# Input i of the second layer as seven block products, with VectorE's order written out through i and g

## The chip, the cores and the metric

One core of a Trainium2 chip runs the whole kernel. The metric is the device time of one execution in microseconds (us). The kernel before takes 673.21 us, the median of three runs (673.01 to 674.18).

## What is computed

A trunk of two layers on 512 tokens of width 1024, in float32. Each layer is `h = h + norm(mixer(norm(h)))`, followed by a gated embedding. Layer 0's mixer is attention, layer 1's is a gated linear recurrence (HGRN2). What the change touches is the input projection of layer 1:

```
u = rms_norm(h, norm_pre[1])
proj = u @ w_in                      # 512x1024 times 1024x4096
q, fl, inp, g = split(proj, 4)       # four blocks of 1024 columns
...
o = recurrence(q, fl, inp)
y = (norm(o) * silu(g)) @ w_out
```

`i` below is `inp`, the third block of columns; `g` is the fourth. Both are wanted with tokens on the partitions ("token major"), and both are 512x1024 times 1024x1024 products.

## The kernel before, in words

**Float32 products.** Every operand is kept as a pair of rounded values, hi and lo. `split` (L272) makes a pair with a copy on ScalarE (hi) and a subtraction on VectorE (lo). `three` (L138) multiplies a pair by a pair in three matmuls: L140 takes hi and w_hi, L141 takes lo and w_hi, L142 takes hi and w_lo. Weights come in chunks of 128x1024: `fetch` (L112) issues a DMA on SyncE's queue, and `load_w` (L117) splits the chunk into w_hi (ScalarE, L273) and w_lo (VectorE, L274). There are two buffers for w_hi and two for w_lo, so that a chunk is split only after the chunk two places before it has been used.

**The normed x.** The norm's factor of each token, `r1`, is not multiplied in ahead of i and g: the products run on `xg = h * gain` (tiles b2h, b2l) and the result is scaled by `r1` while it is moved out of PSUM. For the later products with q and fl, `scaled_norm` (L285) makes the normed x itself, `u` (b1h, b1l), from a factor that `spread` (L255) has laid out over the partitions: one VectorE instruction (un, L288), one ScalarE copy (hi) and one VectorE subtraction (lo) for each of eight slices k.

**The tail of layer 0** (`layer_tail`, L339) makes the new h: the gate is multiplied slice by slice (o = 0 to 7), and `gated` (L387) computes sigmoid, product, sum, then `nxt` makes the slice of xg (L281, L282) and adds its squares to the running sum ss_acc (`Stat.add`, L220). The last four slices come one after the other out of 24 matmuls each (`lin_a`).

**i** is made by `lin_b_tok` (L188) in two halves of 96 matmuls, each half with four chunks of weights that serve 24 matmuls apiece. Between the halves the column sums of ss_acc (L236) give `r1`; `spread` (L259) stands after the first chunk of the second half.

**g** is made by `gates` (L783) with seven products of half-size blocks in place of eight (the Strassen-Winograd scheme, here called p1, p2, p3, p6, p7, p4, p5 in the order of the program). Each product is 24 matmuls on two chunks of weights (12 matmuls apiece) into two PSUM banks out of the ring psB of six (L78). Four of the seven (p3, p6, p7, p5) have sums of x blocks as their operand, the tiles `as`, made by `pair` (L721): two ScalarE scalings, four VectorE sums of 128x256 and a split for each of four k; the sums are made in tsum1, which is then used again for weights. Three of the products have sums of weight blocks: the sums are made in tsum0 and tsum1, by DMAs on GpSimd's queue that add to what is there (`more`, L780) and, once for each of two chunks, by a VectorE addition (L818: t2s = t1 + b22). `plus` (L788) combines the products on VectorE, `end` (L793) scales with `r1` and applies SiLU on ScalarE.

**Order.** Within `tc.manual_schedule(engines=...)` the named engines keep the order of the program; elsewhere a planner orders each engine's instructions. Around i and g only TensorE's order is written out before the change; the tail has a part (L371) in which VectorE's is. `pair` and `scaled_norm` are issued after i's matmuls and before `gates`.

The first product after g is that of fl for head 0 (psA<-b1h,w_f).

Of the kernel before, what the change touches and what calls it, by code (L numbers as in the profile page):

```python
# [10 lines left out]
F32 = mybir.dt.float32  # L11
# [35 lines left out]
def tile_fox_hgrn2(  # L47
# [56 lines left out]
    def col(c):  # L104
        return vecs[:, c:c + 1]
# [230 lines left out]
            with first(o == KT - 1):  # L336
                ac.activation(out=self.zg[o], in_=b, func=AF.Copy, scale=col(C_NPOST[self.layer] + o))

    def layer_tail(layer, h, ah, zg, last=False):  # L339

        st = ah.st = Stat()
        ah.zg, hm = zg, ah.mem
        for g in ah.begun:
            for _ in g:
                pass
        for o in range(len(ah.begun), KT - 1):
            eng = gp if not last and o == len(ah.begun) else ve
            for _ in ah.out(o, load_w(wo[layer, o], eng=eng)):
                pass
        eb = []  # L350
        fill = Fill()
        fill.add(*[ah.embed(o, eb.append) for o in LATE])
        with tc.manual_schedule(engines={PE}):
            for _ in ah.out(KT - 1):
                pass
            st.most()
            fill.run(2)
            with first():
                rs = st.rstd()
            fill.run(4)  # L360
            with first():
                rb = spread(rs, copy=False)
            fill.run()

        ws = [load_w(wgC[layer, c]) for c in range(2)]
        raws = [fetch(wgC[layer, c]) for c in range(2, 4)]

        def low(k):
            ve.tensor_tensor(out=hm[1][k], in0=h[k], in1=hm[0][k].bitcast(F32), op=ALU.subtract)

        with tc.manual_schedule(engines={DVE}):  # L371
            for k in range(KT):
                with first():
                    t = t2("zn")
                    ve.tensor_tensor(out=t, in0=rb, in1=zg[k], op=ALU.mult)
                    ve.tensor_tensor(out=h[k], in0=h[k], in1=t, op=ALU.add)
                    ac.copy(hm[0][k], h[k])
                    if k:
                        low(k - 1)
                if k in (4, 6):  # L380
                    ws.append(load_w(None, raw=raws[k // 2 - 2]))
            with first():
                low(KT - 1)
        for o, b in zip(LATE, eb):
            ac.copy(ah.ple(o), b)

        def gated(o, b, f=slice(0, S)):  # L387
            sg = t2("sgm")[:, f]
            ac.activation(out=sg, in_=b[:, f], func=AF.Sigmoid)  # L389
            ve.tensor_tensor(out=sg, in0=sg, in1=ah.ple(o)[:, f], op=ALU.mult)  # L390
            ve.tensor_tensor(out=h[o][:, f], in0=h[o][:, f], in1=sg, op=ALU.add)
            if last:
                nc.sync.dma_start(out[o][:, f], h[o][:, f])
            else:
                nxt(o)

        if not last:
            xg = pair_big("b2")
            stn = Stat()

            def nxt(o):
                split_scaled(xg[0][o], xg[1][o], h[o], col(C_NPRE[1] + o))
                stn.add(h[o])

        banks = lin_c(ws, hm)
        ws = [load_w(wgA[layer, o]) for o in range(2)]
        for o, b in enumerate(banks):
            gated(o, b)
        for o in range(4, KT):
            w = ws.pop(0)  # L410
            if last and o == KT - 1:

                for i in range(2):
                    f = slice(i * S // 2, (i + 1) * S // 2)
                    b = psA()
                    for k in range(KT):
                        three(b[:, f], (kcols(w[0], k), kcols(w[1], k)), (hm[0][k][:, f], hm[1][k][:, f]), k == 0, k == KT - 1)
                    gated(o, b, f)
            else:
                b = lin_a(w, hm)  # L420
                if o + 2 < KT:
                    ws.append(load_w(wgA[layer, o - 2]))
                gated(o, b)
        return None if last else (xg, stn)
# [293 lines left out]

        return (l1, sums)[q].tile([P, D], F32, name=f"tsum{q}{c}", tag=f"tsum{q}{c}")

    def pair(k):  # L721
        un = []
        for b in (k, k + 4):
            un.append(t2("un"))
# [6 lines left out]
        ve.tensor_tensor(out=sm[:, SM_G, :], in0=a12, in1=sm[:, SM_E, :], op=ALU.add)  # L731
        split(a_sum[0][k], a_sum[1][k], sm)

    xg, st = layer_tail(0, h, ah, slots("b3h", F32))

# [31 lines left out]
                three(banks[t], (hi[:, c], lo[:, c]), (w[0][:, f], w[1][:, f]), k == 0, k == 3)  # L769
        return banks  # L770

    def block(i, j, c):

        return wB1[8 + 4 * j + 2 * i + c]

    def more(dst, ap):

# [2 lines left out]

    CH = range(2)

    def gates(dst):  # L783

        def C(i, j, t):
            return dst[2 * (2 * i + t) + j]
# [5 lines left out]
        def end(i, j):  # L792
            for t in CH:  # L793
                q = 2 * i + t
                ac.activation(out=C(i, j, t), in_=C(i, j, t), func=AF.Silu, scale=r1[:, q:q + 1])

        def loads(raws):
            return [load_w(None, raw=raw) for raw in raws]

        t1 = [tsum(0, c) for c in CH]  # L800
        for c in CH:
            nc.sync.dma_start(t1[c], block(0, 0, c))
        w = loads(t1)
        for c in CH:
            more(t1[c], block(0, 1, c))
        p1 = product((0, 0), w)
        w = [load_w(block(1, 0, c)) for c in CH]
        for t in CH:
            ac.copy(C(1, 0, t), p1[t])
        p2 = product((0, 1), w)  # L810
        b22 = [fetch(block(1, 1, c)) for c in CH]
        w = loads(b22)
        plus(0, 0, p2, (1, 0))
        end(0, 0)
        p3 = product(SM_G, w)
        t2s = [tsum(1, c) for c in CH]
        for c in CH:
            ve.tensor_tensor(out=t2s[c], in0=t1[c], in1=b22[c], op=ALU.add)  # L818
            more(b22[c], block(0, 1, c))
        w = loads(t2s)  # L820
        p6 = product(SM_E, w)
        for c in CH:
            more(t2s[c], block(1, 0, c))
        w = loads(b22)
        plus(1, 0, p6, (1, 0))
        plus(0, 1, p3, (1, 0), ALU.subtract)
        p7 = product(SM_F, w)
        w = loads(t2s)
        plus(1, 1, p7, (1, 0))
        p4 = product((1, 1), w)  # L830
        w = loads(t1)
        plus(1, 0, p4, (1, 1))
        end(1, 0)
        p5 = product(SM_D, w)
        for i in CH:
            plus(i, 1, p5, (i, 1), (ALU.add, ALU.subtract)[i])
            end(i, 1)

    def evac_tok(half, banks):
        for t in range(NT):  # L840
            ac.activation(out=it[2 * t + half], in_=banks[t], func=AF.Copy, scale=r1[:, t:t + 1])

    with tc.manual_schedule(engines={PE}):
        banks = lin_b_tok(wB1[0:4], xg, 0)
        r1 = st.rstd()
        rb = []
        banks1 = lin_b_tok(wB1[4:8], xg, 1, between=lambda: rb.append(spread(r1)))
        evac_tok(0, banks)
        for k in range(4):
            pair(k)  # L850
        evac_tok(1, banks1)
        for k in range(KT):
            scaled_norm(u, k, h[k], C_NPRE[1], rb[0])
        gates(sg)
    att.close()

    y = pair_big("b2")
# [308 lines left out]
    with tc.If(ok > 0) as cmp:  # L1166
        with tc.tile_pool(name="rec", bufs=2) as rp:
            ah = bounded(rp)
        layer_tail(1, h, ah, it, last=True)
    with cmp.Else():  # L1170
        with tc.tile_pool(name="rec", bufs=2) as rp:
            general(rp)
# [6 lines left out]
        for o in EARLY:  # L1179
            for _ in ah.early(o):  # L1180
                pass
        layer_tail(1, h, ah, it, last=True)


_INS = ["xT", "pT", "vec", "wfl", "wA0", "wB0", "wA1", "wB1", "wo", "wgC", "wgA", "wpl"]
# [61 lines left out]
```

## Time and profile before

| | us |
|---|---|
| median of three runs | 673.21 |
| the profiled execution | 673.19 |
| its span, first to last instruction | 671.4 |
| TensorE busy | 654.9 |
| VectorE busy | 462.9 |
| ScalarE busy | 352.5 |

The granted clock of TensorE is 0.998 of full speed over the span. The profiled execution stands within 0.02 us of the median, and 1.8 us of it lie outside the span. In the rows below PE is TensorE, DVE VectorE, ACT ScalarE, POOL GpSimd and SPq SyncE's queue of DMAs. Times are us from the start of the span; a row of the timeline gives start and duration, and in brackets how long the engine was idle before it and what ended that. Durations of neighbours overlap on one engine, so what an instruction takes of the engine is read from one start to the next.

### The profile page before, as it was taken

The numbers are of one execution on the slowest core, as the hardware profiler recorded it, in microseconds if no ns is written. First come the engines' busy times: TensorE is split into PE (matmuls) and PEld (weight loads), VectorE is DVE, ScalarE is ACT, GpSimd is POOL, SyncE is SP. The second block draws the span as 40 slices with busy tenths as digits, with TensorE's granted clock in tenths as the row PEclk, the third lists the DMA queues.
The fourth block names the chain that finished last, engine by engine and source line by source line (L and its number), as shares of the span: only waits on it lengthen the run. The fifth ranks groups of instructions, "written<-read, shape, count | busy, mean of one in ns | idle before, by whom it ended". The sixth has DMA issues, their size and how long they took to land. (4 is left out here: it accounts for less than half of the span.)

```text
span 671.4 us, 8969 instructions
## 1 busy us (share of the span) xinstructions
PE 654.9 (98%) x3202; PEld 544.1 (81%) x3202; DVE 462.9 (69%) x935; ACT 352.5 (52%) x676; POOL 44.6 (7%) x51
## 2 busy tenths in 40 slices
PE   8999999999999998999999997999999998999996
PEld 5888888888888877888888876888888887888885
DVE  7596223888888897337699465669888888333953
ACT  6457223766767685434577454364445455434431
POOL 0101200000000061001000101100010000001000
PEclk9999999999999999999999999999999999999999
DMA  8322336655555575321223335721222224122131
GB/s 283 124 70 65 119 103 189 163 152 133 152 139 139 149 225 166 95 95 38 93 90 97 109 77 122 162 95 62 64 79 80 64 94 144 44 95 95 62 111 51
DMA packets 27156, 75.33 MB, mean 112 GB/s; under 512 B 3872, under 2 KB 4256, under 8 KB 27104
## 3 DMA queue, kind: packets, MB, share of 16 engines
q1 hardware_dynamic: 26240, 71.54, 34.6%
q0 software_dynamic: 864, 3.15, 2.7%
q8 instruction: 27, 0.44, 0.3%
q14 instruction: 25, 0.20, 0.1%
HBM read 59.86 MB, written 2.10 MB: 92 GB/s over the span
## 5 line engine op out<-in xcount | busy, mean ns | idle before, releaser
L140 PE MATMUL psA<-b1h,w_hi 128*128 128x512 f32 (+1 forms) x384 | 154.6, 403 | 0.0
L274 DVE TENSOR_TENSOR w_lo<-w_raw,w_hi 128x1024 fp32r<-128x1024 f32 x89 | 109.1, 1226 | 61.5 <-ACT w_hi L273 56.1
L142 PE MATMUL psA<-b1l,w_hi 128*128 128x512 f32 (+1 forms) x384 | 148.6, 387 | 0.0
L141 PE MATMUL psA<-b1h,w_lo 128*128 128x512 f32 (+1 forms) x384 | 148.2, 386 | 0.2 <-DVE w_lo L274 0.2
L273 ACT CAST w_hi<-w_raw 128x1024 fp32r<-128x1024 f32 x90 | 94.1, 1047 | 39.3 <-PE psB L141 17.2
L142 PEld LDWEIGHTS psA<-b1l,w_hi 128*128 128x128 f32 x384 | 72.1, 188 | 15.1
L140 PEld LDWEIGHTS psA<-b1h,w_hi 128*128 128x128 f32 x384 | 72.3, 188 | 12.9 <-ACT sgm L389 0.7
L141 PEld LDWEIGHTS psA<-b1h,w_lo 128*128 128x128 f32 x384 | 72.4, 189 | 12.7 <-DVE w_lo L274 0.6
L142 PE MATMUL psB<-w_lo,b2h 128*128 128x512 f32 x120 | 46.9, 391 | 2.3 <-DVE w_lo L274 2.3
L621 ACT ACTIVATE pp<-pp,nm 128x128 f32<-128x128 f32 (+3 forms) x64 | 36.2, 565 | 23.0 <-DVE nm L619 22.2
L140 PE MATMUL psB<-w_hi,b2h 128*128 128x512 f32 x120 | 47.2, 395 | 0.0
L141 PE MATMUL psB<-w_hi,b2l 128*128 128x512 f32 x120 | 46.7, 389 | 0.0
L619 DVE CUSTOM_DVE_ANT_0 pp<-psB,cmask 128x128 f32<-128x128 f32 (+3 forms) x64 | 30.7, 479 | 14.5 <-PE psB L638 11.4
L230 DVE TENSOR_TENSOR ss_acc<-ss_acc,sq 128x512 f32<-128x512 f32 x26 | 17.9, 688 | 29.0 <-ACT sq L226 28.8
L140 PE MATMUL psA<-b2h,w_hi 128*128 128x512 f32 x80 | 31.8, 397 | 0.0
L274 DVE TENSOR_TENSOR PTl<-psB,PTh 128x128 fp32r<-128x128 f32 (+3 forms) x64 | 30.8, 481 | 1.0 <-ACT PTh L273 0.8
L142 PE MATMUL psA<-b2l,w_hi 128*128 128x512 f32 x80 | 31.2, 390 | 0.0
L638 PE MATMUL psB<-ident,pp 128*128 128x128 f32 x160 | 28.4, 276 | 2.8 <-DVE pp L624 1.5
L141 PE MATMUL psA<-b2h,w_lo 128*128 128x512 f32 x80 | 31.2, 390 | 0.0
L273 ACT CAST PTh<-psB 128x128 fp32r<-128x128 f32 (+3 forms) x64 | 26.9, 422 | 5.8 <-PE psB L638 4.9
L142 PEld LDWEIGHTS psB<-w_lo,b2h 128*128 128x128 f32 x120 | 22.5, 188 | 7.5 <-DVE w_lo L274 2.7
L624 DVE TENSOR_SCALAR pp<-pp,rden 128x128 f32<-128x128 f32 (+3 forms) x64 | 27.3, 426 | 1.0
(247 smaller groups left out, 1295.0 us busy)
## 6 DMA issues: line engine op xcount, KB each, us to landing
w_raw<-in_wA_dram SPq DMA_DIRECT2D x40, 512.0 KB, 3.3
w_raw<-in_wB_dram SPq DMA_DIRECT2D x19, 512.0 KB, 3.8
w_raw<-in_wo_dram SPq DMA_DIRECT2D x16, 512.0 KB, 4.0
h<-in_xT_dram SPq DMA_DIRECT2D x16, 256.0 KB, 6.3
h<-kh SPq DMA_DIRECT2D x32, 128.0 KB, 2.3
w_raw<-in_wgC_dram SPq DMA_DIRECT2D x8, 512.0 KB
w_raw<-in_wgA_dram SPq DMA_DIRECT2D x8, 512.0 KB, 3.3
h<-qh SPq DMA_DIRECT2D x16, 128.0 KB, 2.3
```

Source lines behind the costliest of these rows:

```text
L140: pe.matmul(out=out_ps, lhsT=sta[0], rhs=mov[0], start=start, stop=False)
L141: pe.matmul(out=out_ps, lhsT=sta[1], rhs=mov[0], start=False, stop=False)
L142: pe.matmul(out=out_ps, lhsT=sta[0], rhs=mov[1], start=False, stop=stop)
L230: ve.tensor_tensor(out=self.acc, in0=self.acc, in1=sq, op=ALU.add)
L273: ins = ac.copy(dst_hi, src)
L274: eng.tensor_tensor(out=dst_lo, in0=src, in1=dst_hi.bitcast(F32), op=ALU.subtract)
L619: ve.tensor_tensor_reduce(out=pp[:, :W], in0=sc[:, :W], in1=cmask[:, S - W:S], op0=ALU.add, op1=ALU.min, scale=1.0, scalar=-NEG, accum_out=nm)
L621: ac.activation(out=pp[:, :W], in_=pp[:, :W], func=AF.Exp, bias=nm, scale=-1.0, accum_out=den)
L624: ve.tensor_scalar(out=pp[:, :W], in0=pp[:, :W], scalar1=rden, scalar2=None, op0=ALU.mult)
L638: pe.transpose(out=tp[:, kt * P:(kt + 1) * P], in_=pp[:, kt * P:(kt + 1) * P], identity=ident)
```

## The change

i is made as g is: `gates` becomes `token_major(m, ...)`, called with m = 0 for i and m = 1 for g. `pair` moves into the tail of layer 0, each k right behind the slice h[k + 4] that it needs; of xg[0..3] only the first half of the tokens is made. t2s is loaded with block (1, 1) and t1 is added to it by an accumulating DMA from SBUF to SBUF, in place of the VectorE addition. `rstd` (the sums over ss_acc) stands after p1 of i, `spread` after p3 of i. `scaled_norm` is issued for two k at a time at four places of g: after p3, p6, p7 and p4. VectorE's order is that of the program through both.

```diff
--- before.py
+++ after.py
@@ -336,8 +336,10 @@
             with first(o == KT - 1):
                 ac.activation(out=self.zg[o], in_=b, func=AF.Copy, scale=col(C_NPOST[self.layer] + o))
 
-    def layer_tail(layer, h, ah, zg, last=False):
+    def layer_tail(layer, h, ah, zg, pair=None):
+        last = pair is None
         st = ah.st = Stat()
         ah.zg, hm = zg, ah.mem
         for g in ah.begun:
@@ -399,8 +401,12 @@
             stn = Stat()
 
             def nxt(o):
-                split_scaled(xg[0][o], xg[1][o], h[o], col(C_NPRE[1] + o))
+                f = slice(0, S // 2 if o < 4 else S)
+                split_scaled(xg[0][o][:, f], xg[1][o][:, f], h[o][:, f], col(C_NPRE[1] + o))
                 stn.add(h[o])
+                if o >= 4:
+                    pair(h, o - 4)
 
         banks = lin_c(ws, hm)
         ws = [load_w(wgA[layer, o]) for o in range(2)]
@@ -718,7 +724,7 @@
 
         return (l1, sums)[q].tile([P, D], F32, name=f"tsum{q}{c}", tag=f"tsum{q}{c}")
 
-    def pair(k):
+    def pair(h, k):
         un = []
         for b in (k, k + 4):
             un.append(t2("un"))
@@ -731,7 +737,7 @@
         ve.tensor_tensor(out=sm[:, SM_G, :], in0=a12, in1=sm[:, SM_E, :], op=ALU.add)
         split(a_sum[0][k], a_sum[1][k], sm)
 
-    xg, st = layer_tail(0, h, ah, slots("b3h", F32))
+    xg, st = layer_tail(0, h, ah, slots("b3h", F32), pair)
 
 
 
@@ -769,9 +775,9 @@
                 three(banks[t], (hi[:, c], lo[:, c]), (w[0][:, f], w[1][:, f]), k == 0, k == 3)
         return banks
 
-    def block(i, j, c):
-        return wB1[8 + 4 * j + 2 * i + c]
+    def block(m, i, j, c):
+        return wB1[8 * m + 4 * j + 2 * i + c]
 
     def more(dst, ap):
 
@@ -780,7 +786,7 @@
 
     CH = range(2)
 
-    def gates(dst):
+    def token_major(m, dst, between=None):
 
         def C(i, j, t):
             return dst[2 * (2 * i + t) + j]
@@ -792,66 +798,80 @@
         def end(i, j):
             for t in CH:
                 q = 2 * i + t
-                ac.activation(out=C(i, j, t), in_=C(i, j, t), func=AF.Silu, scale=r1[:, q:q + 1])
+                ac.activation(out=C(i, j, t), in_=C(i, j, t), func=AF.Silu if m else AF.Copy, scale=r1[:, q:q + 1])
 
         def loads(raws):
             return [load_w(None, raw=raw) for raw in raws]
 
         t1 = [tsum(0, c) for c in CH]
+        t2s = [tsum(1, c) for c in CH]
         for c in CH:
-            nc.sync.dma_start(t1[c], block(0, 0, c))
+            nc.sync.dma_start(t1[c], block(m, 0, 0, c))
         w = loads(t1)
         for c in CH:
-            more(t1[c], block(0, 1, c))
+            more(t1[c], block(m, 0, 1, c))
         p1 = product((0, 0), w)
-        w = [load_w(block(1, 0, c)) for c in CH]
+        w = [load_w(block(m, 1, 0, c)) for c in CH]
+        if between:
+            between(0)
         for t in CH:
             ac.copy(C(1, 0, t), p1[t])
         p2 = product((0, 1), w)
-        b22 = [fetch(block(1, 1, c)) for c in CH]
+        b22 = [fetch(block(m, 1, 1, c)) for c in CH]
         w = loads(b22)
+        for c in CH:
+            nc.sync.dma_start(t2s[c], block(m, 1, 1, c))
+            more(t2s[c], t1[c])
         plus(0, 0, p2, (1, 0))
         end(0, 0)
         p3 = product(SM_G, w)
-        t2s = [tsum(1, c) for c in CH]
         for c in CH:
-            ve.tensor_tensor(out=t2s[c], in0=t1[c], in1=b22[c], op=ALU.add)
-            more(b22[c], block(0, 1, c))
+            more(b22[c], block(m, 0, 1, c))
         w = loads(t2s)
+        if between:
+            between(1)
         p6 = product(SM_E, w)
         for c in CH:
-            more(t2s[c], block(1, 0, c))
+            more(t2s[c], block(m, 1, 0, c))
         w = loads(b22)
         plus(1, 0, p6, (1, 0))
         plus(0, 1, p3, (1, 0), ALU.subtract)
+        if between:
+            between(2)
         p7 = product(SM_F, w)
         w = loads(t2s)
         plus(1, 1, p7, (1, 0))
+        if between:
+            between(3)
         p4 = product((1, 1), w)
         w = loads(t1)
         plus(1, 0, p4, (1, 1))
         end(1, 0)
+        if between:
+            between(4)
         p5 = product(SM_D, w)
         for i in CH:
             plus(i, 1, p5, (i, 1), (ALU.add, ALU.subtract)[i])
             end(i, 1)
 
-    def evac_tok(half, banks):
-        for t in range(NT):
-            ac.activation(out=it[2 * t + half], in_=banks[t], func=AF.Copy, scale=r1[:, t:t + 1])
-    with tc.manual_schedule(engines={PE}):
-        banks = lin_b_tok(wB1[0:4], xg, 0)
-        r1 = st.rstd()
-        rb = []
-        banks1 = lin_b_tok(wB1[4:8], xg, 1, between=lambda: rb.append(spread(r1)))
-        evac_tok(0, banks)
-        for k in range(4):
-            pair(k)
-        evac_tok(1, banks1)
-        for k in range(KT):
+    r1 = None
+    rb = []
+    def beside_i(n):
+        nonlocal r1
+        if n == 0:
+            r1 = st.rstd()
+        if n == 1:
+            rb.append(spread(r1))
+    def beside_g(n):
+        for k in ((), (0, 1), (2, 3), (4, 5), (6, 7))[n]:
             scaled_norm(u, k, h[k], C_NPRE[1], rb[0])
-        gates(sg)
+    with tc.manual_schedule(engines={PE, DVE}):
+        token_major(0, it, beside_i)
+        token_major(1, sg, beside_g)
     att.close()
 
     y = pair_big("b2")
@@ -1166,7 +1186,7 @@
     with tc.If(ok > 0) as cmp:
         with tc.tile_pool(name="rec", bufs=2) as rp:
             ah = bounded(rp)
-        layer_tail(1, h, ah, it, last=True)
+        layer_tail(1, h, ah, it)
     with cmp.Else():
         with tc.tile_pool(name="rec", bufs=2) as rp:
             general(rp)
@@ -1179,7 +1199,7 @@
         for o in EARLY:
             for _ in ah.early(o):
                 pass
-        layer_tail(1, h, ah, it, last=True)
+        layer_tail(1, h, ah, it)
 
 
 _INS = ["xT", "pT", "vec", "wfl", "wA0", "wB0", "wA1", "wB1", "wo", "wgC", "wgA", "wpl"]
```

## Rows read from the trace of the kernel before

**Rows 1.** The page, busy time of the engines.

```profile
PE 654.9 (98%) x3202; PEld 544.1 (81%) x3202; DVE 462.9 (69%) x935; ACT 352.5 (52%) x676; POOL 44.6 (7%) x51
```

**Rows 2.** Windows i, g: length; PE, PEld, DVE, ACT, POOL busy; clock; DMA.

```profile
353.20:399.05 45.85, 45.84 (x210) 37.89 (x209) 33.17 (x51) 27.97 (x40) 3.01 (x2) 1.00 0.31 94
399.05:442.20 43.15, 39.12 (x169) 31.26 (x168) 26.12 (x27) 19.95 (x23) 4.47 (x6) 1.00 0.55 123
```

**Rows 3.** Waits of TensorE in both windows: total, times, longest.

```profile
PE psB L142 <- DVE w_lo L274: 4.0, 2, 2.3
```

**Rows 4.** Timeline of VectorE before those two waits.

```profile
402.14 1.23 DVE L818 TENSOR_TENSOR tsum<-tsum,w_raw 128x1024 f32<-128x1024 f32 x1 [5.36 <-DMA tsum<-in_wB_dram]
403.28 1.22 DVE L274 TENSOR_TENSOR w_lo<-tsum,w_hi 128x1024 fp32r<-128x1024 f32 x1
404.42 1.22 DVE L274 TENSOR_TENSOR w_lo<-w_raw,w_hi 128x1024 fp32r<-128x1024 f32 x1
...
412.31 1.23 DVE L818 TENSOR_TENSOR tsum<-tsum,w_raw 128x1024 f32<-128x1024 f32 x1 [3.05 <-DMA w_raw<-in_wB_dram]
```

**Rows 5.** Timeline of TensorE: i, then g's p3.

```profile
373.67 0.39 PE L142 MATMUL psA<-w_lo,b2h 128*128 128x512 f32 x1
...
375.03 0.39 PE L142 MATMUL psB<-w_lo,b2h 128*128 128x512 f32 x1
375.26 0.95 PE L236 MATMUL psB<-ones,ss_acc 128*128 128x1 f32 x8
...
415.06 0.39 PE L140 MATMUL psB<-w_hi,as 128*128 128x512 f32 x1
...
416.69 0.40 PE L141 MATMUL psB<-w_hi,as 128*128 128x512 f32 x1
```

**Rows 6.** Window of the tail of layer 0, columns as in group 2.

```profile
331.80:357.90 26.10, 26.09 (x115) 21.25 (x115) 25.73 (x39) 19.49 (x31) 0.00 (x0) 1.00 0.25 83
```

**Rows 7.** Timeline of VectorE, end of the tail and the block sums.

```profile
357.26 0.69 DVE L230 TENSOR_TENSOR ss_acc<-ss_acc,sq 128x512 f32<-128x512 f32 x1
357.86 0.41 DVE L728 TENSOR_TENSOR tsum<-un 128x256 f32<-128x256 f32 x1
358.19 0.42 DVE L730 TENSOR_TENSOR tsum<-un 128x256 f32<-128x256 f32 x1
...
370.22 1.22 DVE L274 TENSOR_TENSOR as<-tsum,as 128x1024 fp32r<-128x1024 f32 x1 [1.11 <-ACT as L273]
```

**Rows 8.** Lines of VectorE in the tail: xg's low parts, busy, mean ns.

```profile
L282 DVE SCALAR_TENSOR_TENSOR b2l<-h,vecs,b2h 128x512 fp32r<-128x512 f32 x8 | 6.0, 745 | 0.2 <-ACT b2h L281 0.2
```

**Rows 9.** Timeline of VectorE in the part whose order is written out.

```profile
316.14 1.22 DVE L274 TENSOR_TENSOR w_lo<-w_raw,w_hi 128x1024 fp32r<-128x1024 f32 x1 [0.31 <-ACT w_hi L273]
317.28 0.68 DVE L375 TENSOR_TENSOR zn<-psB,b3h 128x512 f32<-128x512 f32 x1
```

**Rows 10.** Timeline of ScalarE and VectorE: one chunk's split in g.

```profile
417.18 1.05 ACT L273 CAST w_hi<-tsum 128x1024 fp32r<-128x1024 f32 x1 [0.53 <-PE psB L141]
418.26 1.22 DVE L274 TENSOR_TENSOR w_lo<-tsum,w_hi 128x1024 fp32r<-128x1024 f32 x1 [1.26 <-ACT w_hi L273]
```

**Rows 11.** Timeline of VectorE and ScalarE: g's last additions, slices of u.

```profile
441.73 2.48 DVE L790 TENSOR_TENSOR b3l<-psB,b3l 128x512 f32<-128x512 f32 x4 [0.99 <-PE psB L142]
...
392.57 1.41 DVE L288 SCALAR_TENSOR_TENSOR un<-h,vecs,rbc 128x512 f32<-128x512 f32 x2
393.35 0.62 ACT L273 CAST b1h<-un 128x512 fp32r<-128x512 f32 x1 [2.70 <-DVE un L288]
394.00 0.69 DVE L274 TENSOR_TENSOR b1l<-un,b1h 128x512 fp32r<-128x512 f32 x1
```

**Rows 12.** DMA issues: count, KB each, median us to landing; below L778's own.

```profile
tsum<-in_wB_dram SPq DMA_DIRECT2D x2, 512.0 KB, 3.6
h<-kh SPq DMA_DIRECT2D x32, 128.0 KB, 2.3
...
DMA to landing us min/median/max: 5.3/5.9/6.8
```

## The prediction, made before the change was run

> **What bounds the kernel now.** I read the page first: TensorE is busy 98% of the span, VectorE 69%, ScalarE 52% [rows 1]. So time is saved where matmuls go or where TensorE stands still, and lost where it is made to wait. Next the windows of the two stages that change: i takes 45.85 us without a gap, g 43.15 us of which TensorE is busy 39.12 [rows 2]. The waits of TensorE name the whole gap: twice L142 waits for a w_lo, 4.0 us together [rows 3]. The timeline of VectorE shows why: both times the addition L818 stands at the head of VectorE, idle until a DMA lands (5.36 and 3.05 us), and the w_lo that TensorE needs is behind it [rows 4].
>
> **The sum, part by part**, against the profiled execution's 673.19 us (span 671.4; the median of the runs is 673.21).
>
> *Matmuls, -4.8.* On plain x blocks six matmuls take 373.67 to 375.03, 0.227 us each; on the sums `as` seven take 415.06 to 416.69, 0.233 each [rows 5]. i has 192 plain ones, 43.5 us. As seven products it has 72 plain and 96 on sums: 16.3 + 22.4 = 38.7. The sums and the spread of the norm only change places on TensorE.
>
> *The additions L818, -4.0.* Both waits go with them [rows 3]. What is late next are the splits on VectorE, now in a fixed order. That such an order is kept although other work is ready shows in the tail: the w_lo at 316.14 was waited for with VectorE idle 0.31 us, and the next slice came behind it [rows 9].
>
> *The start of i, +6.0.* VectorE is busy 25.73 of the last 26.10 us of the tail [rows 6], and the last squares reach ss_acc at 357.26, ready by 357.9 [rows 7]. The block sums came after that, until 371.4 [rows 7]. Now three of the four `pair`s stand ahead of it in the program. One is four sums at 0.33 (357.86 to 358.19 [rows 7]) and a split at 1.14 (403.28 to 404.42 [rows 4]), 2.5 us; three are 7.4. The halved slices of xg give back four times about 0.3 (half of 0.745 less what does not shrink [rows 8]), 1.2. That makes 364.1, and up to one more chunk split of 1.1 slips between. The column sums L236 are now due right after p1, at 353.2 + 24 x 0.227 = 358.6; before they stood at 375.26 [rows 5] and had time. TensorE stops for 5.5 to 6.6; I take 6.0. Below, it is 0 if the planner lets the pairs fall behind the tail as before; above, 7.4 if nothing is given back.
>
> *p6 of i, +0.7.* t2s shares tsum1 with the last two pairs. The last squares at 364.7, then the last pair's sums 1.3, its ScalarE copy 1.05, its split 1.2 and one chunk split between: 369.5. Then a plain DMA of 3.6 and an accumulating one of 5.9 [rows 12], 379.0, and the chunk's split, 1.05 on ScalarE and 1.22 on VectorE with the signals [rows 10]: 381.4. p2 starts at 365.5, p3 at 370.9, p6 at 377.5 (1.0 for the spread), and needs its second w_lo at 380.7. No row shows an accumulating DMA from SBUF to SBUF. Below, it could take the 2.3 us of a plain 128 KB copy inside SBUF, and nothing is late; above, the slowest accumulation and that copy one after the other, 6.8 + 2.3, and p6 is 3.9 late. I take 5.9, the same bytes on the same queue. The Trainium skill (DMA: Bandwidth & Descriptors, Anatomy of one DMA — SWDGE (gpsimd) path) gives such a transfer 2.0 us and its bytes at 436 GB/s, for 512 KB 3.2 us as an estimate; by that the 0.7 goes and the sum is 685.2; the accumulations in the trace are 2.1 us or more above it.
>
> *p7 of i, +3.5.* The banks go round a ring of six. `rstd` and `spread` each take one inside i, so p7's second bank is p3's first, which is free when `plus` has read it. In program order that addition stands behind both splits of p7's weights and two additions for p6. The second split starts when p6's last matmul frees its buffer: about 2.4 us past p7's due start [rows 10]. Three additions at 0.62 (four take 2.48 [rows 11]) make 4.2; TensorE wants the bank after three matmuls, at 0.7. Bounds 0, if the ring hands out another bank, and 3.6.
>
> *From i to g, +2.8.* p5's four additions, 2.48 [rows 11], now stand on VectorE ahead of g's first w_lo, 1.22 [rows 10]. The first two start 0.7 before p5 ends, so w_lo is there 3.2 after the end with the signals; it is wanted 0.45 after it. The chunk's own load has to wait for the last split out of tsum0 in i and takes 3.6 [rows 12]; it lands inside p5 and is not the last. Bounds 0 and 3.3.
>
> *The slices of u beside g, +8.5.* Before, they ran beside i, where VectorE had room, batched in threes. In order, one slice is un, the copy on ScalarE, then the subtraction: 392.57 to 394.00 and 0.60 more [rows 11], 2.0 us; two are 4.1. In a product VectorE has little room: the second chunk's w_lo is done 2.4 past its start, and the next product's first w_lo must start by 5.6 + 0.47 - 1.22 = 4.85. After p3 two slices fill 2.4 to 6.5: p7 is 1.65 late. Then the second split, four additions (2.5) and two slices: 3.4 late for p4. Then the split, two additions and two slices: 2.3 late for p5. That is 7.3 with ScalarE always free. Where a w_hi of 1.05 [rows 10] goes ahead of a slice's copy, about 1 is added at each of three places, 10.5 at most. I take 8.5. The last two slices are covered by p5, since fl uses u slice by slice.
>
> *At nothing.* `r1` is wanted first by `end` after p2, the spread norm by the slices after g's p3. SyncE issues sixteen loads for i and g in place of fourteen, GpSimd sixteen accumulations in place of six; the DMA share of 0.31 and 0.55 [rows 2] has room, and but for p6 (above) each lands a product ahead. Cover gone, each would cost its lateness, as at p6.
>
> Sum: -4.8 - 4.0 + 6.0 + 0.7 + 3.5 + 2.8 + 8.5 = +12.7, **685.9 us**. The stage after g is as it was and gives nothing back, so the delay goes to the end.
>
> **The rivals.**
>
> *The order costs nothing.* VectorE is busy 26.12 of 43.15 us in g [rows 2]; if it and ScalarE reach every w_lo before the 4.85 us in each product, and the tail lets the pairs fall behind, only the first two terms stay: 673.19 - 8.8 = 664.4. For it speaks the mean share; against it the position of the slices and additions right ahead of the splits. It decides where a w_lo starts less than 4.85 us into a product.
>
> *The pairs fall behind the tail's own work.* The planner put a ready sum late before [rows 7], and may again: the start costs 0 and the sum is 679.9. Against it, they now stand earlier in the program than the last slice.
>
> *i's splits wait for the whole tail.* If the written order begins only when all of the tail's VectorE work is done (369.5), p1's first w_lo comes at 370.7, wanted at 353.65: 17.0 in place of 6.0 + 0.7, 696.2. Against it: nothing in the program says so.
>
> *VectorE's order is not kept.* Then the splits go ahead of the additions, the slices fill gaps, and p7, g and part of the rest do not wait: -8.8 + 6.0 + 0.7 and at most 2.8 for loads into tsum0, about 673.9, no change. Against it [rows 9].
>
> **How the numbers follow.** The forecast has a chance of 0.58, the pairs behind 0.22, the order at no cost 0.12, the wait for the whole tail 0.05, the order not kept 0.03. The forecast with its low ends (5.5, 0, 3.5, 2.3, 7.3) gives +9.8, without the ring's 3.5 +6.3; with its high ends (7.4, 3.9, 3.6, 3.3, 10.5) +19.9; the pairs behind with low ends +4.3, 677.5. The range 677.0 to 692.0 takes in the forecast but for all its high ends at once and the second case, and leaves out the other three, 0.20. About 0.2% is what a measurement of this kernel can tell from no change. Faster by more is the first rival, 0.12; within it the last, 0.03; slower 0.85.
>
> **What would show it.** Right: TensorE idle ahead of L236 for 5 to 7 us, ended by ss_acc; ahead of p7's fourth matmul in i for 3 to 4, ended by an addition of `plus`; ahead of L142 at g's start for about 3 and at three products of g for 1.6 to 3.5 each, ended by w_lo; the window of i at 51 to 55 us and of g's seven products at 46 to 50. Wrong: both windows near 39 to 41 without gaps, or w_lo starting in the first 4.8 us of each product.

## The result and the profile after

The changed kernel takes **697.93 us** (median of 4 runs, 697.19 to 700.15); the kernel before, on the same chip, 673.12 (673.01 to 674.18). The ratio is 1.0376, with a 95% interval of 1.0359 to 1.0393: slower by 24.8 us. The profiled execution took 698.36 us, span 696.6, so the difference of the two profiled executions is +25.2. Forecast was +12.7: the direction is right, the size is half, and the time lies outside the range.

From the page of the changed kernel: busy time of the engines, and the granted clock of TensorE in 40 slices:

```profile
PE 663.0 (95%) x3178; PEld 547.2 (79%) x3178; DVE 474.8 (68%) x953; ACT 358.3 (51%) x684; POOL 52.3 (8%) x61
PEclk9999999999999999999989899889999999999999
```

TensorE has 24 instructions fewer than before and is busy 8.1 us longer [rows 1]. Fewer matmuls of the same shape can only take longer if each is slower, and the second line hints at it: four slices, all of them between 348 and 470 us, are below 9. The windows of i and of g, columns as in group 2 of the rows before:

```profile
353.12:410.50 57.38, 47.85 (x185) 36.98 (x184) 34.51 (x46) 26.68 (x33) 8.12 (x9) 0.88 0.68 165
410.50:467.98 57.48, 46.24 (x171) 35.82 (x170) 36.54 (x46) 26.27 (x33) 7.03 (x9) 0.88 0.53 119
```

i grew from 45.85 to 57.38 us and g from 43.15 to 57.48 [rows 2]; the clock was 1.00 in both, now it is 0.88. From the first matmul of fl to the end of the span it is 228.6 us, before 229.1: all of the loss lies in these two windows. The waits of TensorE there (total, times, longest), and then each long one on its timeline:

```profile
PE psB L142 <- DVE w_lo L274: 16.5, 7, 2.9
PE psB L140 <- ACT w_hi L273: 4.2, 2, 3.5
```
```profile
355.91 0.50 PE L142 MATMUL psB<-w_lo,b2h 128*128 128x512 f32 x1 [2.16 <-DVE w_lo L274]
...
363.13 0.72 PE L142 MATMUL psB<-w_lo,b2h 128*128 128x512 f32 x1 [2.60 <-DVE w_lo L274]
...
388.19 0.79 PE L140 MATMUL psB<-w_hi,as 128*128 128x512 f32 x1 [3.53 <-ACT w_hi L273]
...
394.39 0.39 PE L142 MATMUL psB<-w_lo,as 128*128 128x512 f32 x1
394.62 0.40 PE L140 MATMUL psB<-w_hi,as 128*128 128x512 f32 x1
...
413.87 0.50 PE L142 MATMUL psB<-w_lo,b2h 128*128 128x512 f32 x1 [2.65 <-DVE w_lo L274]
...
440.72 0.50 PE L142 MATMUL psB<-w_lo,as 128*128 128x512 f32 x1 [2.86 <-DVE w_lo L274]
...
450.99 0.50 PE L142 MATMUL psB<-w_lo,b2h 128*128 128x512 f32 x1 [2.87 <-DVE w_lo L274]
...
452.05 0.63 PE L140 MATMUL psB<-w_hi,b2h 128*128 128x512 f32 x1
452.47 0.63 PE L141 MATMUL psB<-w_hi,b2l 128*128 128x512 f32 x1
...
456.34 0.39 PE L140 MATMUL psB<-w_hi,b2h 128*128 128x512 f32 x1
456.57 0.39 PE L141 MATMUL psB<-w_hi,b2l 128*128 128x512 f32 x1
...
461.20 0.50 PE L142 MATMUL psB<-w_lo,as 128*128 128x512 f32 x1 [2.87 <-DVE w_lo L274]
```

Seven long waits and two short ones (0.66 and 0.53, in p6 of i) make 20.7 us. The prediction's terms for waits come to 21.5. But look at what follows a wait: the matmuls at 452.05 and 452.47 start 0.42 apart, those at 456.34 and 456.57 0.23 apart. Windows over these two places, and first over the matmuls right behind the wait:

```profile
450.99:451.95 0.96, 0.96 (x4) 0.82 (x5) 0.96 (x1) 0.00 (x0) 0.00 (x0) 1.00 0.00 0
452.00:455.40 3.40, 3.40 (x9) 2.63 (x8) 1.93 (x4) 0.94 (x1) 0.00 (x0) 0.50 0.00 0
456.00:457.60 1.60, 1.60 (x9) 1.33 (x8) 1.36 (x2) 0.03 (x1) 0.21 (x1) 1.00 0.00 0
```

Right behind the wait the clock is still 1.00, 2.4 GHz; from 452.00 TensorE is granted 0.50, which is 1.2 GHz; at 456.00 it has 1.00 again. Each of the seven long waits has such a slow stretch with it, 27.3 us together. In six cases the stretch begins 0.1 to 1.0 us after the wait's end; in p6 of i it begins 1.1 us before it. **The account** at the first matmul of fl, 467.98 against 442.22: matmuls -4.8, waits 20.7 - 4.0 = +16.7, and the clock: of the 27.3 us at half speed 1.1 lie inside a wait that is counted already, the other 26.2 lose half, +13.1. That is 25.0; measured is 25.8. Of the 0.8 left most is at the restarts: the first two matmuls behind a wait start 0.33 to 0.34 apart at full clock in place of 0.23, and there are nine waits in place of two.

### The profile page after: what moved, and what is told of

Its sections match the earlier page's. It is cut to its first block, busy times and chain, and to the rows that moved or that the text cites. A ratio compares the mean times of both kernels' runs of the same rounds, so it can differ in the third digit from the quotient of the medians.

```text
span 696.6 us, 8998 instructions
## 1 busy us (share of the span) xinstructions
PE 663.0 (95%) x3178; PEld 547.2 (79%) x3178; DVE 474.8 (68%) x953; ACT 358.3 (51%) x684; POOL 52.3 (8%) x61
## 5 line engine op out<-in xcount | busy, mean ns | idle before, releaser
L274 DVE TENSOR_TENSOR w_lo<-w_raw,w_hi 128x1024 fp32r<-128x1024 f32 x87 | 106.6, 1227 | 67.3 <-ACT w_hi L273 67.1
L273 ACT CAST w_hi<-w_raw 128x1024 fp32r<-128x1024 f32 x88 | 92.1, 1048 | 41.6 <-PE psB L141 22.3
L142 PEld LDWEIGHTS psA<-b1l,w_hi 128*128 128x128 f32 x384 | 72.1, 188 | 15.1
L142 PE MATMUL psB<-w_lo,b2h 128*128 128x512 f32 x96 | 40.4, 421 | 10.3 <-DVE w_lo L274 10.3
L140 PE MATMUL psB<-w_hi,b2h 128*128 128x512 f32 x96 | 40.1, 419 | 0.0
L141 PE MATMUL psB<-w_hi,b2l 128*128 128x512 f32 x96 | 40.0, 416 | 0.0
L273 ACT CAST w_hi<-tsum 128x1024 fp32r<-128x1024 f32 x16 | 16.7, 1044 | 35.1 <-PE psB L141 20.0
L142 PE MATMUL psB<-w_lo,as 128*128 128x512 f32 x64 | 27.7, 433 | 6.3 <-DVE w_lo L274 6.3
L142 PEld LDWEIGHTS psB<-w_lo,b2h 128*128 128x128 f32 x96 | 19.6, 204 | 16.4 <-DVE w_lo L274 12.0
L140 PE MATMUL psB<-w_hi,as 128*128 128x512 f32 x64 | 28.0, 437 | 4.2 <-ACT w_hi L273 4.2
```

The source lines that it names most:

```text
L140: pe.matmul(out=out_ps, lhsT=sta[0], rhs=mov[0], start=start, stop=False)
L141: pe.matmul(out=out_ps, lhsT=sta[1], rhs=mov[0], start=False, stop=False)
L142: pe.matmul(out=out_ps, lhsT=sta[0], rhs=mov[1], start=False, stop=stop)
L273: ins = ac.copy(dst_hi, src)
L274: eng.tensor_tensor(out=dst_lo, in0=src, in1=dst_hi.bitcast(F32), op=ALU.subtract)
```

## The experiments

Each kernel was timed beside the kernel before on its own chip, and ratios are to that. "Waits" are those of TensorE from the start of i to fl. The parts that the runs take away share waits and slow stretches with one another, so what they give back is not to be added up.

### Is it the clock? Matmuls in place of the waits

`e1_warm`: just ahead of the matmuls that wait, matmuls on zeros are issued into a bank that nobody reads (added work), as many as fill the wait.

```diff
-        p1 = product((0, 0), w)
+        p1 = product((0, 0), w, ({(0, 2): 9, (2, 2): 11}, {(0, 2): 11})[m])
...
+    def warm(n):
+        if n:
+            b = psA()
+            for _ in range(n):
+                pe.matmul(out=b, lhsT=idle[:, 0:P], rhs=idle, start=True, stop=True)
...
```

> Matmuls on zeros into a spare bank are put into TensorE's order at the nine places where it waited in i and g, about as many as fill each wait; nothing else changes. Theory A (the waits cost their 20.7 us and the fall of the granted clock behind them another 12.9 us of slow matmuls): the clock stays at its upper level, the slow matmuls go, part of it comes back as longer waits because TensorE reaches the late splits sooner: 684 to 691 us. Rival B (the fall of the clock lies under the waits and costs nothing of its own): 697 to 700 us.

Measured: 691.56 us, ratio 1.0282 (1.0260 to 1.0305), span 688.8 against 696.6. The window from i to fl and the waits in it:

```profile
353.10:457.90 104.80, 101.07 (x434) 71.77 (x439) 70.01 (x90) 52.38 (x65) 15.16 (x18) 1.00 0.64 151
```
```profile
PE psB L144 <- DVE w_lo L276: 2.4, 7, 0.5
PE psB L140 <- ACT w_hi L275: 1.0, 2, 0.8
```

With TensorE kept at work the clock is 1.00, and fl starts 10.1 us sooner (457.90 for 467.98), though no other engine was given less to do: the clock's fall is a cost of its own. It is 3.0 less than the 13.1 of the account. A slow TensorE also asks for the next w_lo later, so at full clock part of the gain comes back as waiting, here mostly filled: the added matmuls are busy for 19.5 us and 3.4 us of waits are left, 22.9 beside the 20.7 of the changed kernel. That is 2.2 of the 3.0; no run measures it alone. In the span 7.8 of the 10.1 stay, since fl to the end now takes 230.9; by the ratios of the two kernels the gain is 0.9%, 6.3 us. The time is just above the 684 to 691 of the clock theory, and far below the rival's 697.

### Which part makes which wait?

`e4_slices_free`: the slices of u are left to the planner; the written order holds for i and for g apart.

```diff
...
     with tc.manual_schedule(engines={PE, DVE}):
         token_major(0, it, beside_i)
-        token_major(1, sg, beside_g)
+    for k in range(KT):
+        scaled_norm(u, k, h[k], C_NPRE[1], rb[0])
+    with tc.manual_schedule(engines={PE, DVE}):
+        token_major(1, sg)
```

> The eight slices of u are issued between i and g and are free of the written order; the rest of VectorE's order is kept. Theory A (g's three waits of 2.9 us are the slices in front of the splits): those waits and the half clock behind them go, 8.6 + 3 x 1.7 = 13.7 us, and a few us of others may come: 684 to 688 us. Rival B (the additions and splits alone make g late): at least two of the waits stay and the time is above 692 us.

685.70 us, ratio 1.0190 (1.0169 to 1.0210), as expected, span 12.5 less than that of the changed kernel. The waits:

```profile
PE psB L142 <- DVE w_lo L274: 8.8, 4, 4.0
PE psB L140 <- ACT w_hi L273: 3.0, 1, 3.0
```

The three waits inside g are gone; the one at g's start grew from 2.65 to 3.97. In all the waits fall from 20.7 to 11.8 us, and the time at half clock only from 27.3 to 20.5, because the stretches at g's start and at the second wait of p1 are now 6.8 us long each: 8.9 + 3.4 = 12.3. So the slices beside g made the three waits, and about a quarter of what they cost is clock.

`e3_t2_add`: t2s is again a VectorE addition, in the written order after p3; the plain load and the accumulation inside SBUF go.

```diff
-        for c in CH:
-            nc.sync.dma_start(t2s[c], block(m, 1, 1, c))
-            more(t2s[c], t1[c])
...
+            ve.tensor_tensor(out=t2s[c], in0=t1[c], in1=b22[c], op=ALU.add)
```

> The sum t2s is made by the VectorE addition again, after p3 in the written order; the load and the accumulating DMA inside SBUF go. Theory A (p6 of i waits for that accumulating DMA): p6's waits (0.7, 0.5 and 3.5 us) and the 6.8 us of half clock behind them go, 8.1 us together; the two additions of 1.14 us put the first split of p6 about 1.1 us late in i and in g: 692 us. Rival B (p6 waits for VectorE's order or for a PSUM bank): p6's wait stays and the time is 697 us or more.

690.44 us, ratio 1.0251 (1.0216 to 1.0285), span -7.8, a little below the 692 expected. p6's wait in i falls from 4.7 in all to 0.3 and its slow stretch of 6.8 goes. g's waits hardly change in sum (2.64, 0.53, 1.12, 3.32, 2.87), but one of them is now two short ones, and its slow stretch of 3.4 goes too. So the DMA sum costs a wait and its slow stretch.

`e6_pairs_late`: the pairs stand behind the tail, as before, and the planner places them.

```diff
-                if o >= 4:
-                    pair(h, o - 4)
...
     xg, st = layer_tail(0, h, ah, slots("b3h", F32), pair)
+    for k in range(4):
+        pair(h, k)
```

> The four pairs are issued behind the tail, as before the change, and are free of the written order; all else as after. Theory A (the pairs in the tail hold up p1's splits): the two waits in p1 (2.2 and 2.6 us) and the two half-clock stretches behind them (1.7 us each) go, 8.2 us; but the block sums then end no earlier while p6 comes earlier, so that p6's wait for t2s grows from 3.5 to about 8 us: net 692 to 697 us. Rival B (p1 is late for another reason, its load or ScalarE): both waits in p1 stay, 697 us or more.

699.42 us, ratio 1.0398 (1.0369 to 1.0427), no better than the changed kernel and above the 692 to 697 expected. The two waits at the start only shrink, 2.16 and 2.60 to 1.44 and 1.79, and the sums that come later make t2s later:

```profile
PE psB L142 <- DVE w_lo L274: 14.5, 6, 2.9
PE psB L140 <- ACT w_hi L273: 8.9, 1, 8.9
```

Only 1.5 of the 4.8 us at the start are the pairs'; neither theory had that. Moved early, the pairs saved p6 more than they cost p1.

`e5_free_order`: nothing but VectorE's order is given back to the planner.

```diff
-    with tc.manual_schedule(engines={PE, DVE}):
+    with tc.manual_schedule(engines={PE}):
```

> Only TensorE's order is written out; VectorE is ordered by the planner; all else as after the change. Theory A (VectorE's written order costs the wait between i and g and the three in g, 11.3 us, and four half-clock stretches of 1.7 us): 680 us, with the waits at the start of i and at p6 of i still there, up to 683 if a load into tsum0 is late. Rival B (the pairs in the tail and the DMA chain carry most of it): above 690 us.

682.83 us, ratio 1.0152 (1.0123 to 1.0181), span -15.1, as expected. The written order is worth about 15 of the 25 us. The start (2.19 and 2.20) and p6 of g (2.75, with a slow stretch) still wait.

`e7_three_undone`: e6, e3 and e4 together; VectorE's order stays written out for splits and additions.

> Pairs behind the tail, t2s by the VectorE addition, slices of u free: three parts undone, i as seven products and VectorE's order of splits and additions kept. Theory A (the parts were the cost and the order of splits and additions leaves only the wait between i and g): 673.2 - 8.8 and then 2.7 to 4 us of waiting at g's start with 1.7 of half clock, 1 us for each addition ahead of p6's split: 670 to 676 us. Rival B (the order as such is the cost): above 680 us.

682.16 us, ratio 1.0131 (1.0110 to 1.0152): the rival's range. With nothing but splits and additions in the order TensorE still waits 4.0 us at g's start, with a slow stretch of 6.8, beside 1.44 and 1.79 at the start of i. With the order free (`e5_free_order`) the wait at g's start was 0.47.

### Why does VectorE reach w_lo late in g?

The timeline of VectorE and of ScalarE in the changed kernel, ahead of the wait at 450.99:

```profile
441.72 2.48 DVE L796 TENSOR_TENSOR b3l<-psB,b3l 128x512 f32<-128x512 f32 x4
444.12 0.74 DVE L288 SCALAR_TENSOR_TENSOR un<-h,vecs,rbc 128x512 f32<-128x512 f32 x1
445.78 0.69 DVE L274 TENSOR_TENSOR b1l<-un,b1h 128x512 fp32r<-128x512 f32 x1 [0.92 <-ACT b1h L273]
446.39 0.75 DVE L288 SCALAR_TENSOR_TENSOR un<-h,vecs,rbc 128x512 f32<-128x512 f32 x1
449.11 0.69 DVE L274 TENSOR_TENSOR b1l<-un,b1h 128x512 fp32r<-128x512 f32 x1 [1.98 <-ACT b1h L273]
449.72 2.35 DVE L274 TENSOR_TENSOR w_lo<-tsum,w_hi 128x1024 fp32r<-128x1024 f32 x2
```
```profile
447.51 1.05 ACT L273 CAST w_hi<-tsum 128x1024 fp32r<-128x1024 f32 x1 [1.77 <-issue]
448.46 0.61 ACT L273 CAST b1h<-un 128x512 fp32r<-128x512 f32 x1
```

VectorE works 5.1 us and stands 2.9 us idle between 441.72 and 449.72, each time for the copy b1h, and the second copy stands behind a w_hi on ScalarE. The w_lo that TensorE wants is the first of the two in the last row. Two kernels take this apart.

`g2_two_un_first`: both un of a portion first, then both splits.

```diff
+        uns = []
         for k in ((), (0, 1), (2, 3), (4, 5), (6, 7))[n]:
-            scaled_norm(u, k, h[k], C_NPRE[1], rb[0])
+            uns.append((k, t2("un")))
+            ve.scalar_tensor_tensor(out=uns[-1][1], in0=h[k], scalar=col(C_NPRE[1] + k), in1=rb[0], op0=ALU.mult, op1=ALU.mult)
+        for k, un in uns:
+            split(u[0][k], u[1][k], un)
```

> After the change, with the two slices of a portion made un, un, then low, low, so that VectorE does not stand still through the first copy on ScalarE. Theory A (the standing still between un and low is what is too long): each portion is 1.4 us or more shorter, the three waits in g fall to about 1.5 us and their half clock goes: 687 to 692 us. Rival B (VectorE's work without the standing still is already too much): waits of 2.5 us or more stay, 695 us or more.

691.19 us, ratio 1.0257 (1.0235 to 1.0279), within the range expected, though not in its parts: the three waits become 0.72, 2.87 and none, so one stays as it was, and p6 of i waits longer (5.59).

`g1_scalar_order`: ScalarE's order is written out too.

```diff
-    with tc.manual_schedule(engines={PE, DVE}):
+    with tc.manual_schedule(engines={PE, DVE, mybir.EngineType.Activation}):
```

> After the change, with ScalarE's order written out through i and g as well, so that a slice's copy stands ahead of the next chunk's w_hi. Theory A (a w_hi that waits for TensorE's buffer stands ahead of the slice's copy, and so VectorE waits for TensorE while TensorE waits for VectorE): VectorE's waits for b1h fall to about 0.7 us each, the three waits in g from 2.9 to about 2 us, 690 to 695 us. Rival B (VectorE's own work per product sets g's pace): the three waits stay at 2.9 us, 697 us or more.

695.60 us, ratio 1.0328 (1.0304 to 1.0353), just above what was expected. What VectorE waited for in g (total, times, longest):

```profile
DVE w_lo L274 <- ACT w_hi L273: 13.7, 10, 4.2
DVE b1l L274 <- ACT b1h L273: 4.1, 6, 0.7
```

In the changed kernel the waits for b1h were 9.1 in six, the longest 2.1. They fall to 0.7 each, so the long ones did come from ScalarE's order. But now the w_hi are late: TensorE waits 3.70 at g's start and 2.43 later for one. An order written by hand on one more engine moved the wait.

### Does it help to want w_lo later?

`f1_low_last`: the changed kernel, with the twelve matmuls of a weight chunk reordered: four that use w_hi with the high parts, four with the low parts, the four with w_lo last. w_lo is wanted six matmuls, 1.36 us, later.

```diff
-        for k in range(4):
-            w, f = ws[k // 2], slice(k % 2 * S, (k % 2 + 1) * S)
...
+        for part in range(2):
+            w = ws[part]
+            for q in range(3):
+                for j in range(2):
+                    k, f = 2 * part + j, slice(j * S, (j + 1) * S)
+                    x = operand(kind, k)[q == 1]
+                    for t in range(2):
+                        pe.matmul(out=banks[t], lhsT=x[:, t * P:(t + 1) * P], rhs=w[q == 2][:, f], start=k == 0 and q == 0, stop=k == 3 and q == 2)
```

> After the change, with one thing altered: in each product the matmuls of a chunk run in the order hi, lo, then those with w_lo, so that a w_lo is wanted 1.36 us later. Theory A (the waits are splits 2 to 3 us late, each with a fall of the clock behind it, and waits of about 1.4 us have none): seven waits lose 1.36 us each and six half-clock stretches of 1.7 us go, 678 us; VectorE's full order beside g gives some of it back, up to 687; p6's wait for its DMA stays. Rival B (VectorE's work sets g's pace, so that any slack is used up): 692 us or more.

695.66 us, ratio 1.0343 (1.0318 to 1.0367): the rival. Of g's four waits two fall to 1.64 and 1.55, two stay at 2.90 and 2.83, and p6 of i grows to 6.59: where VectorE's chain or the DMA sets the pace, it hardly matters when TensorE asks.

`f4_before_low_last`: the same edit in the products of the kernel before.

> The kernel before with the same order of matmuls in g's products and nothing else. Theory A: its two waits of 2.3 and 1.7 us shrink by 1.36 us each: 670.0 to 671.0 us; i as seven products is then worth the rest of the best version's lead, up to 4.8 us. Rival B (the waits were ended by DMAs and stay as long): 672.5 to 673.5 us.

673.10 us, ratio 1.0000 (0.9990 to 1.0011). The two waits of [rows 3] fall from 4.0 to 2.6 in all, less than expected, and nothing of it shows in the time.

### Is there a version of i as seven products that gains?

`b3_vector_add`: the pairs in i, behind p1 and the sums of L236; VectorE's order free; t2s by a VectorE addition. `b2_gpsimd_add` is the same with that addition on GpSimd.

```diff
-                if o >= 4:
-                    pair(h, o - 4)
...
-        for c in CH:
-            nc.sync.dma_start(t2s[c], block(m, 1, 1, c))
-            more(t2s[c], t1[c])
...
+            ve.tensor_tensor(out=t2s[c], in0=t1[c], in1=b22[c], op=ALU.add)
...
             r1 = st.rstd()
+            for k in range(4):
+                pair(h, k)
...
-    with tc.manual_schedule(engines={PE, DVE}):
+    with tc.manual_schedule(engines={PE}):
```

> i as seven products, the pairs issued behind p1 and the sums L236, only TensorE's order written out, the sum t2s made by a GpSimd addition. Theory A: neither the pairs, nor the DMA inside SBUF, nor a VectorE instruction that waits for a DMA stands ahead of a split, so 664 to 669 us, faster than both kernels. Rival B (the clock falls at any short wait, or GpSimd's additions hold VectorE up): 673 us or more.

> As the run with GpSimd's addition, but the sum t2s on VectorE as before the change, placed by the planner. Theory A: the two waits for DMAs of the kernel before (4.0 us) come in g and perhaps also in i, without a fall of the clock: 667 to 673 us. Rival B (i as seven products gains nothing even without the other parts): 673 us or more.

Measured 676.57 us on GpSimd, ratio 1.0052 (1.0034 to 1.0069), and 675.25 on VectorE, 1.0033 (1.0016 to 1.0050): 20 us and more given back, yet above the time expected and no gain over the kernel before. b3's longest wait is 2.65 at g's start, with a slow stretch. A GpSimd addition took 2.88 us in the mean of four, against 1.23 on VectorE [rows 4].

`f2_best`: b3 with w_lo last in each chunk. `f3_dma_sum`: f2, with t2s again by the accumulating DMA inside SBUF.

> i as seven products, pairs behind p1, VectorE free of a written order, t2s by the VectorE addition, and the matmuls with w_lo last in each chunk. Theory A: the five waits of 0.5 to 2.7 us that this version has without the last point shrink below 1.4 us or go, and so does its half-clock stretch: 664 to 668 us, faster than before. Rival B (block sums and additions keep VectorE late in i): 671 us or more.

> As the best version, but t2s by the accumulating DMA inside SBUF. Theory A (that DMA takes 7 to 9.5 us after the pairs and after t1 has landed): p6 waits about 4 to 8 us in i with a fall of the clock, and up to 3 us in g: 671 to 679 us, slower than with the addition. Rival B (with VectorE free the sums come early enough): within 1 us of the version with the addition.

f2: **669.79 us** (median of 7 runs, 668.53 to 671.45), ratio 0.9952 (0.9935 to 0.9968): faster than both kernels, by 0.5% than the kernel before, though above the 664 to 668 expected. With VectorE free, then, the later w_lo is worth something: from b3 to f2 the ratio falls by 0.8%. Its window from i to fl and its waits:

```profile
353.10:438.70 85.60, 82.17 (x353) 65.92 (x352) 75.33 (x98) 54.74 (x69) 19.71 (x14) 0.98 0.60 138
```
```profile
PE psB L775 <- ACT as L273: 2.0, 1, 2.0
PE psB L236 <- DVE ss_acc L230: 1.3, 1, 1.3
```

The account is made as above: matmuls -4.8, waits 3.3 - 4.0 = -0.7, one slow stretch +1.7, sum -3.8; fl starts 3.5 sooner than in the kernel before. VectorE is busy 75.33 of 85.60 us, 88%, so little room is left on it.

f3: 684.48 us, ratio 1.0179 (1.0156 to 1.0202), 14.7 above f2, more than was expected:

```profile
PE psB L775 <- ACT w_hi L273: 11.3, 3, 8.1
PE psB L775 <- ACT as L273: 2.0, 1, 2.0
```

8.1 us of the waits is p6 of i, which stands for t2s with a slow stretch of 10.2 us, about half of it inside the wait. The DMA sum cost time in both surroundings tried (e3, f3).

## Why the prediction failed, step by step

**The step that failed is a term that is not there.** The sum counted each wait at its length. The kernel before had two waits, and the clock in its windows is 1.00 [rows 2], so nothing was put in for what TensorE does after one. Here the clock fell to 1.2 GHz at each long wait: 13.1 us in the account; taken away in e1 it gave back 10.1 at fl, 7.8 in the span and 6.3 by the ratios, of the 12.0 by which the forecast of 685.9 was exceeded. Without it the account is -4.8 + 16.7 = +11.9, beside a forecast of +12.7; no term for the clock was in the range either, so its upper end, 692, lay below the time. The windows foretold, 51 to 55 us for i and 46 to 50 for g, came out at 57.4 and 57.5, with 6.3 and 6.8 us of clock in them.

The terms one by one:

- *Matmuls, -4.8*: right, by the count (24 fewer) and by the spacing at full clock, 0.23, but for the restarts behind waits.
- *Additions, -4.0*: right, both waits of [rows 3, 4] are gone.
- *Start of i, +6.0*: 4.8, but at another place. L236 did not wait at all; TensorE stood earlier, at p1's two w_lo:

```profile
353.97 0.42 DVE L737 TENSOR_TENSOR tsum<-un,tsum 128x256 f32<-128x256 f32 x1
354.31 0.41 DVE L736 TENSOR_TENSOR tsum<-un 128x256 f32<-128x256 f32 x1
354.64 1.22 DVE L274 TENSOR_TENSOR w_lo<-tsum,w_hi 128x1024 fp32r<-128x1024 f32 x1
355.85 1.23 DVE L274 TENSOR_TENSOR as<-tsum,as 128x1024 fp32r<-128x1024 f32 x1
...
361.51 0.42 DVE L736 TENSOR_TENSOR tsum<-un 128x256 f32<-128x256 f32 x1 [0.96 <-ACT un L731]
361.85 1.22 DVE L274 TENSOR_TENSOR w_lo<-tsum,w_hi 128x1024 fp32r<-128x1024 f32 x1
```

  The splits stand among the tail's own work and the pairs' sums; a chunk of weights serves twelve matmuls, 2.7 us, and VectorE is full. The prediction asked when the column sums come and not when each w_lo does. By e6 the pairs are 1.5 of the 4.8; that the rest is the tail's own work and the shorter use of each chunk is argued from this timeline, and no run takes it apart. The upper bound of 7.4 does not follow from the term's own numbers: sums ready at 357.9 + 7.4 and due at 358.6 make 6.7, or 7.8 with the chunk split.
- *p6 of i, +0.7*: mis-sized, 4.7. For the second chunk the plain load could start at 372.1, not 369.5, took 5.0 and not 3.6, and the accumulation 9.4 and not 5.9. ScalarE and GpSimd show it:

```profile
377.63 0.86 POOL L784 DMA_DIRECT2D tsum<-tsum  x1 [0.43 <-issue]
387.09 1.04 ACT L273 CAST w_hi<-tsum 128x1024 fp32r<-128x1024 f32 x1 [4.64 <-DMA tsum<-tsum]
```

  The upper bound given was 3.9. The 3.2 us that are estimated for these bytes from the Trainium skill (DMA: Bandwidth & Descriptors, Anatomy of one DMA — SWDGE (gpsimd) path) are not what any of the four took (7.1 to 9.4).
- *p7 of i, +3.5*: wrong. Its second bank is entered at 394.62, 0.23 after the matmul before, with no wait. The additions that read p6's and then p3's banks came only after that:

```profile
395.91 0.68 DVE L796 TENSOR_TENSOR b3h<-psB,b3h 128x512 f32<-128x512 f32 x1
```

  So the bank was not p3's first, as the prediction had it; it was another, the case of the term's lower bound.
- *i to g, +2.8*: 2.65, right.
- *Slices beside g, +8.5*: 2.86 + 2.87 + 2.87 = 8.6, right in sum; the parts forecast were 1.65, 3.4 and 2.3 before the extra for ScalarE. That extra is there (0.92 and 1.98 above, and g1).

So errors of the waits nearly cancelled (p6 +4.0; start -1.2 and p7 -3.5): that 20.7 us of waits stand beside 21.5 forecast is luck. The clock came on top. Of the rivals, "the order is not kept" was priced at 673.9 at most, and e5, which takes just that away, gave 682.8. Its price had waits of 9.5 us in it, at the start of i, p6 of i and the loads; e5 had 10.4, of which 2.75 at p6 of g, where nothing was foreseen. What the price left out is again the clock, 0.93 from i to fl in e5, about 7 us. What "at nothing" claimed of `r1`, the spread and the other loads holds in so far as none of them ends a wait. But the room on the DMA queues that it claimed was small: the DMA share in i rose from 0.31 to 0.68, and p6's transfers took longer than in the kernel before.

## What to carry to other kernels

Price a wait of TensorE by its length and by the granted clock behind it: here 16.7 us of added waiting brought a loss of 13.1 us to the clock with them, while the 4.0 us of waits in the kernel before brought none. Before an order is written out for a second engine, follow each operand of TensorE back through every engine in it, with the point at which it is wanted; a mean busy share of 64% (VectorE in g) did not tell what the position of each w_lo told. An exchange of an addition for a DMA frees the engine and lengthens the chain; where the result is wanted soon, as t2s is in p6, the addition was better in both places tried.

## What was not expected of the hardware

- The clock. In the changed kernel waits of 2.16 to 3.53 us each had a stretch at 1.2 GHz with them, six of 3.4 us and one, in p6, of 6.8; its waits of 0.5 to 0.7 alone had none. In the kernel before the waits of 2.32 and 1.71 had none [rows 2, 3]. In other kernels waits of 1.79 (e7) and 2.00 (f2) had one, of 1.64 (f1), 2.12 (the second in g1) and 2.19 (in g of f3) not, and in f1 one came behind waits of 1.53 and 1.38. So the wait's length alone does not decide here; what does was not settled. The Trainium skill (TensorE: Matmul & The Clock Gate, HAM oscillation — how this bites in real kernels) tells of a kernel that waits for data before each group of matmuls and then runs the group at the low clock. The window at 452.00 agrees with that, but the one at 450.99 shows the first matmuls behind the wait still at the upper level, and the waits of the kernel before had no slow stretch at all.
- The accumulating DMA from SBUF to SBUF took 7.1 and 9.4 us in i and 8.6 and 8.9 in g, against 5.3 to 6.8 for those that read HBM in the kernel before [rows 12]. The source alone does not make the difference. In the changed kernel those that read HBM are slow too (GpSimd's queue, i and g, last column the median):

```profile
tsum<-in_wB_dram POOLq DMA_DIRECT2D x8, 512.0 KB, 7.3
tsum<-tsum POOLq DMA_DIRECT2D x4, 512.0 KB, 8.8
w_raw<-in_wB_dram POOLq DMA_DIRECT2D x4, 512.0 KB, 8.1
```

  In f3 the four inside SBUF had a median of 5.5, those from HBM 6.0 and 8.1. Sixteen such transfers run in i and g in place of six; that their number is the cause was not tried by itself.
